# Two rows of each sum on ScalarE, and the first stores behind the last load, in a row-wise dot product with softmax

## The chip, the cores and the metric

The kernel runs on one core of one Trainium2 chip. The metric is the device time of one execution in microseconds (us). A profile gives the span of one profiled execution, which is about 2 us shorter than its device time. Times quoted are medians of runs.

## The reference

```python
B, N, D = 8, 4096, 512                                # x, y: float32
gram = np.matmul(x, y.transpose(0, 2, 1))
diag = np.diagonal(gram, axis1=1, axis2=2)            # only row n of x with row n of y
diag = diag - diag.max(axis=-1, keepdims=True)
exp = np.exp(diag)
return (exp / exp.sum(axis=-1, keepdims=True)).astype(np.float32)
```

Only the diagonal is needed: 8 x 4096 dot products of length 512, then a softmax over 4096 of them, eight times. All of x and y is read once, 134.2 MB; the output has 131 KB.

## The kernel before

The 8 rows of the output are done as two sets of four. Each set is four steps of 32 rows a partition, eight steps in all. x has two buffers, y has one. In the first six steps (`S - 2`) VectorE multiplies all rows with two instructions and sums them with a third. ScalarE's only large work there is a copy of the last six rows of y, so that the y buffer is free as soon as the first product ends. The last two steps use fused multiply-and-sum instructions row by row, with ever smaller loads.

```python
    # R = 32 rows a step, K = 6, C // R = 4 steps a set, G = 32, P = 128
    for t in range(S - 2):
        load_x(t, 0, R)                      # waits for the sum of step t - 2
        load_y(t, 0, R)                      # waits for the first product of step t - 1
        nc.scalar.activation(out=side, in_=ys[:, R - K :, :], func=Act.Copy)
        products(t, 0, R - K, ys[:, : R - K, :])
        if t == C // R:
            store(0, sump, G)                # first set: sum, reciprocal, scale, four stores
        products(t, R - K, K, side)
        sums(t, 0, R)                        # one VectorE reduce of 32 rows
        if t == C // R - 1:
            sump = exps(0, diag[0])
    # ... step 6: y in two halves, fused dots; step 7: loads of 16, 8, 4, 2, 1, 1 rows, fused dots ...
    store(1, exps(1, diag[1][:, C - 2 :]), P)

    def store(i, sump, n):
        # ... total, reciprocal, scaling on VectorE ...
        for p in range(0, P, n):
            nc.scalar.dma_start(out=ov[i, p : p + n, :], in_=res[i][p : p + n, :])
```

All loads are issued by SP, the SyncE engine, in program order. An issue puts a load into SP's queue; the load lands when its last byte is in the buffer.

Of the kernel before, what the change touches and what calls it, by code (L numbers as in the profile page):

```python
# [1 line left out]

# [5 lines left out]


@with_exitstack
def kernel(
    ctx: ExitStack,
    tc: tile.TileContext,
    x: bass.AP,
    y: bass.AP,
    out: bass.AP,
):
    nc = tc.nc
    ctx.enter_context(tc.manual_schedule())  # L20
    f32 = mybir.dt.float32
    Alu = mybir.AluOpType
    Act = mybir.ActivationFunctionType
    X = mybir.AxisListType.X
    B, N, D = x.shape
    P = nc.NUM_PARTITIONS
    G = 32
    Q = P // G
    C = N // G
    R = 32  # L30
    H = R // 2
    K = 6
    S = B // Q * (C // R)


    xv = x.rearrange("(s b) (j c) d -> s (b j) c d", b=Q, j=G)
    yv = y.rearrange("(s b) (j c) d -> s (b j) c d", b=Q, j=G)
    ov = out.rearrange("(s b) (j c) -> s (b j) c", b=Q, j=G)

    big = ctx.enter_context(tc.tile_pool(name="big", bufs=1))  # L40
    small = ctx.enter_context(tc.tile_pool(name="small", bufs=1))


    xs = [big.tile([P, R, D], f32, name=f"xs{i}") for i in range(2)]
    ys = big.tile([P, R, D], f32, name="ys")
    side = big.tile([P, K, D], f32, name="side")

    diag = [small.tile([P, C + 2 * i], f32, name=f"diag{i}") for i in range(B // Q)]
    res = [small.tile([P, C], f32, name=f"res{i}") for i in range(B // Q)]

    def columns(t, r0, n):
        c0 = t % (C // R) * R + r0
        return slice(c0, c0 + n)

    def rows(t, r0, n):
        return xs[t % 2][:, r0 : r0 + n, :]

    def dots_of(t, r0, n):
        return diag[t * R // C][:, columns(t, r0, n)]

    def load_x(t, r0, n):
        nc.sync.dma_start(out=rows(t, r0, n), in_=xv[t * R // C, :, columns(t, r0, n), :])  # L62

    def load_y(t, r0, n):
        nc.sync.dma_start(out=ys[:, r0 : r0 + n, :], in_=yv[t * R // C, :, columns(t, r0, n), :])  # L65

    def products(t, r0, n, yt):
        xt = rows(t, r0, n)
        nc.vector.tensor_tensor(out=xt, in0=xt, in1=yt, op=Alu.mult)  # L69

    def sums(t, r0, n):
        nc.vector.tensor_reduce(out=dots_of(t, r0, n), in_=rows(t, r0, n), axis=X, op=Alu.add)  # L72

    def dots(t, r0, n):
        for r in range(r0, r0 + n):
            xt = xs[t % 2][:, r, :]
            nc.vector.scalar_tensor_tensor(  # L77
                out=xt, in0=xt, scalar=1.0, in1=ys[:, r, :], op0=Alu.mult, op1=Alu.mult,
                accum_out=dots_of(t, r, 1),
            )  # L80

    def over_quadrant(name, column, op, negate=False):

        got = small.tile([P, 1], f32, name=name)
        nc.vector.tensor_reduce(  # L85
            out=got, in_=column.to_broadcast([P, G]), axis=X, op=op, negate=negate, apply_transpose=True
        )
        return got

    def largest(out, d):  # L90
        nc.vector.tensor_reduce(out=out, in_=d, axis=X, op=Alu.max)  # L91

    def exps(i, d):
        mxp = small.tile([P, 1], f32, name=f"mxp{i}")
        largest(mxp, d)
        nmx = over_quadrant(f"nmx{i}", mxp, Alu.max, negate=True)
        sump = small.tile([P, 1], f32, name=f"sump{i}")
        nc.scalar.activation(out=res[i], in_=diag[i][:, :C], func=Act.Exp, bias=nmx, scale=1.0, accum_out=sump)  # L98
        return sump

    def store(i, sump, n):
        total = over_quadrant(f"sum{i}", sump, Alu.add)
        rc = small.tile([P, 1], f32, name=f"rc{i}")
        nc.vector.reciprocal(out=rc, in_=total)  # L104
        nc.vector.tensor_single_scalar(out=res[i], in_=res[i], scalar=rc, op=Alu.mult)  # L105
        for p in range(0, P, n):
            nc.scalar.dma_start(out=ov[i, p : p + n, :], in_=res[i][p : p + n, :])

    for t in range(S - 2):
        load_x(t, 0, R)  # L110
        load_y(t, 0, R)
        nc.scalar.activation(out=side, in_=ys[:, R - K :, :], func=Act.Copy)  # L112
        products(t, 0, R - K, ys[:, : R - K, :])
        if t == C // R:
            store(0, sump, G)
        products(t, R - K, K, side)
        sums(t, 0, R)
        if t == C // R - 1:
            sump = exps(0, diag[0])

    t = S - 2
    load_x(t, 0, R)
    for r0 in (0, H):
        load_y(t, r0, H)
        dots(t, r0, H)

    t += 1
    r0 = 0
    for n in (16, 8, 4, 2, 1, 1):
        load_x(t, r0, n)  # L130
        load_y(t, r0, n)
        if r0 == 0:
            largest(diag[1][:, C : C + 1], diag[1][:, : C - R])
        if r0 == R - 2:
            largest(diag[1][:, C + 1 :], diag[1][:, C - R : C - 2])
        dots(t, r0, n)
        r0 += n
    store(1, exps(1, diag[1][:, C - 2 :]), P)


# [1 line left out]
_INS = ['x', 'y']  # L142
_OUTS = [((8, 4096), 'float32')]


# [23 lines left out]
```

## Time and profile before

| | before |
|---|---|
| three runs | 321.05 to 321.68 us, median 321.35 |
| span of the profiled run | 319.5 us |
| VectorE busy | 249.1 us (78%) |
| ScalarE busy | 18.9 us (6%) |
| load queue's share of the 16 DMA engines | 97.6% |
| one step | 38.7 us, 16.78 MB, 433 GB/s |

### The profile page before, as it was taken

What the parts mean: (1) busy time and instruction counts of PE and PEld (TensorE: products, weight loads), DVE (VectorE), ACT (ScalarE), POOL (GpSimd) and SP (SyncE); (2) the same over time, 40 slices, a digit from 0 to 9 for tenths busy, and PEclk for the clock granted to TensorE, in tenths of its full rate; (3) what the DMA queues carried; (4) which work ended last, traced back from release to release, by engine and by line L of the source; (5) the groups of instructions that cost most, each with busy time, mean ns of one, the idle gap of its engine ahead of it and who ended that gap; (6) DMA issues with size and microseconds to landing.
All of it is one profiled execution on the core that took longest, in us unless ns stands there. A gap on an engine that the chain in (4) does not pass through costs nothing.

```text
span 319.5 us, 284 instructions
## 1 busy us (share of the span) xinstructions
DVE 249.1 (78%) x158; ACT 18.9 (6%) x11; POOL 0.2 (0%) x4
## 2 busy tenths in 40 slices
DVE  0000079996899949999499995999959999994995
ACT  1000030000300003000120003000030000000000
POOL 0000000000000000000000000000000000000000
DMA  9999999999999999999999999999999999999992
GB/s 394 394 394 517 402 394 484 435 394 468 435 410 394 492 427 394 484 435 394 435 476 402 394 509 410 394 492 429 396 414 484 390 419 447 415 431 410 424 411 101
DMA packets 4225, 134.36 MB, mean 421 GB/s; under 512 B 512, under 2 KB 768, under 8 KB 1536
## 3 DMA queue, kind: packets, MB, share of 16 engines
q1 hardware_dynamic: 3888, 134.22, 97.6%
q10 hardware_dynamic: 336, 0.13, 0.1%
q14 instruction: 1, 0.01, 0.0%
HBM read 134.22 MB, written 0.13 MB: 421 GB/s over the span
## 4 chain that ended last, share of the span: by engine, by line
DMA 60%; DVE 36%; issue 2%; SPq 0%; ACT 0%; DVEq 0%
DMA ys<-in_y_dram 60%; DVE xs L69 27%; DVE xs L77 5%; DVE diag L72 4%; SPq L62 0%; DVE res L105 0%; DVE sum L85 0%; DVE nmx L85 0%; ACT res L98 0%; DVE rc L104 0%; DVE mxp L91 0%; SPq L65 0%; DVEq L69 0%; DVEq L77 0%
## 5 line engine op out<-in xcount | busy, mean ns | idle before, releaser
L69 DVE TENSOR_TENSOR xs<-xs,ys 128x13312 f32<-128x13312 f32 x6 | 84.2, 14025 | 62.3 <-DMA ys<-in_y_dram 62.3
L72 DVE TENSOR_REDUCE diag<-xs 128x32 f32<-128x16384 f32 x6 | 103.3, 17220 | 0.2
L77 DVE SCALAR_TENSOR_TENSOR xs<-xs,ys 128x512 f32<-128x512 f32 x64 | 39.6, 685 | 4.6 <-DMA ys<-in_y_dram 4.5
L112 ACT ACTIVATE side<-ys 128x3072 f32<-128x3072 f32 x6 | 16.6, 2765 | 187.5 <-DMA ys<-in_y_dram 151.4
L69 DVE TENSOR_TENSOR xs<-xs,side 128x3072 f32<-128x3072 f32 x6 | 20.1, 3351 | 0.0
L98 ACT ACTIVATE res<-diag,nmx 128x128 f32<-128x128 f32 x2 | 0.8, 402 | 109.2 <-DVE nmx L85 109.2
L77 DVE DVE_READ_ACCUMULATOR xs<-xs,ys 128x1 f32 x64 | 5.2, 81 | 0.0
L112 ACT ACT_TABLE_LOAD x1 | 1.3, 1283 | 0.7 <-PEq L153 0.7
L85 DVE TRANSPOSE_TENSOR_REDUCE sum<-sump 128x1 f32<-128x32 f32 x2 | 0.4, 208 | 0.6 <-ACT res L98 0.6
L105 DVE TENSOR_SCALAR res<-res,rc 128x128 f32<-128x128 f32 x2 | 0.6, 287 | 0.1
L91 DVE TENSOR_REDUCE mxp<-diag 128x1 f32<-128x128 f32 (+1 forms) x2 | 0.4, 222 | 0.1
L91 DVE TENSOR_REDUCE diag<-diag 128x1 f32<-128x96 f32 (+1 forms) x2 | 0.4, 218 | 0.1
L85 DVE TRANSPOSE_TENSOR_REDUCE nmx<-mxp 128x1 f32<-128x32 f32 x2 | 0.4, 212 | 0.1
L104 DVE RECIPROCAL rc<-sum 128x1 f32<-128x1 f32 x2 | 0.3, 164 | 0.1
L98 ACT ACTIVATION_READ_ACCUMULATOR res<-diag,nmx 128x1 f32 x2 | 0.4, 187 | 0.0
L153 POOL MEMSET const-uint8-127<- 128x1 uint8 x1 | 0.1, 103 | 0.0
L153 POOL MEMSET const-bfloat16-1.0<- 128x1 bf16 x1 | 0.1, 102 | 0.0
L153 POOL MEMSET const-float32-0.0<- 128x1 f32 x1 | 0.1, 99 | 0.2 <-issue 0.2
L153 POOL MEMSET const-float32-1.0<- 128x1 f32 x1 | 0.1, 99 | 0.0
## 6 DMA issues: line engine op xcount, KB each, us to landing
ys<-in_y_dram SPq DMA_DIRECT2D x3, 4096.0 KB, 14.9
xs<-in_x_dram SPq DMA_DIRECT2D x1, 4096.0 KB, 14.1
xs<-in_x_dram SPq DMA_DIRECT2D x1, 2048.0 KB, 18.5
ys<-in_y_dram SPq DMA_DIRECT2D x1, 2048.0 KB, 18.9
xs<-in_x_dram SPq DMA_DIRECT2D x1, 1024.0 KB, 21.0
ys<-in_y_dram SPq DMA_DIRECT2D x1, 1024.0 KB, 21.4
xs<-in_x_dram SPq DMA_DIRECT2D x1, 512.0 KB, 22.3
ys<-in_y_dram SPq DMA_DIRECT2D x1, 512.0 KB, 22.8
```

The lines of the kernel that those rows point to most:

```text
L69: nc.vector.tensor_tensor(out=xt, in0=xt, in1=yt, op=Alu.mult)
L72: nc.vector.tensor_reduce(out=dots_of(t, r0, n), in_=rows(t, r0, n), axis=X, op=Alu.add)
L77: nc.vector.scalar_tensor_tensor(out=xt, in0=xt, scalar=1.0, in1=ys[:, r, :], op0=Alu.mult, op1=Alu.mult, accum_out=dots_of(t, r, 1),)
L85: nc.vector.tensor_reduce(out=got, in_=column.to_broadcast([P, G]), axis=X, op=op, negate=negate, apply_transpose=True)
L91: nc.vector.tensor_reduce(out=out, in_=d, axis=X, op=Alu.max)
L98: nc.scalar.activation(out=res[i], in_=diag[i][:, :C], func=Act.Exp, bias=nmx, scale=1.0, accum_out=sump)
L104: nc.vector.reciprocal(out=rc, in_=total)
L105: nc.vector.tensor_single_scalar(out=res[i], in_=res[i], scalar=rc, op=Alu.mult)
L112: nc.scalar.activation(out=side, in_=ys[:, R - K :, :], func=Act.Copy)
L153: nc = _bacc.Bacc("TRN2", target_bir_lowering=False, num_devices=1)
```

## The change

Its intent is to take work off VectorE, so that x buffers come free earlier, and to take the four small stores of the first set out of the stream of loads, to a place behind it.

```diff
+    W = 2
...
+    def sums_act(t, r0, n):
+        for r in range(r0, r0 + n):
+            row = xs[t % 2][:, r, :]
+            nc.scalar.activation(out=row, in_=row, func=Act.Copy, accum_out=dots_of(t, r, 1))
...
-    def store(i, sump, n):
+    def normalize(i, sump):
         # ... total, reciprocal, scaling as before ...
-        for p in range(0, P, n):
-            nc.scalar.dma_start(out=ov[i, p : p + n, :], in_=res[i][p : p + n, :])
...
         if t == C // R:
-            store(0, sump, G)
+            normalize(0, sump)
         products(t, R - K, K, side)
-        sums(t, 0, R)
+        sums(t, 0, R - W)
+        sums_act(t, R - W, W)
...
-    store(1, exps(1, diag[1][:, C - 2 :]), P)
+
+    for p in range(0, P, G):
+        nc.sync.dma_start(out=ov[0, p : p + G, :], in_=res[0][p : p + G, :])
+    normalize(1, exps(1, diag[1][:, C - 2 :]))
+    nc.scalar.dma_start(out=ov[1], in_=res[1])
```

## The prediction

> **What bounds the kernel now.** I read the page first for who is busy, then the windows for the rate of the loads step by step, then the timeline of one step for when loads are issued and land, then the waits of the load queue, then the tail.
>
> The page's parts 2, 3 and 5, of the kernel before. The queue rows give packets, MB and the share of 16 engines' span; the group rows give busy time, mean ns of one, and idle time ahead of it.
> ```profile
> DMA  9999999999999999999999999999999999999992
> ...
> q1 hardware_dynamic: 3888, 134.22, 97.6%
> q10 hardware_dynamic: 336, 0.13, 0.1%
> ...
> L69 DVE TENSOR_TENSOR xs<-xs,ys 128x13312 f32<-128x13312 f32 x6 | 84.2, 14025 | 62.3 <-DMA ys<-in_y_dram 62.3
> L72 DVE TENSOR_REDUCE diag<-xs 128x32 f32<-128x16384 f32 x6 | 103.3, 17220 | 0.2
> L112 ACT ACTIVATE side<-ys 128x3072 f32<-128x3072 f32 x6 | 16.6, 2765 | 187.5 <-DMA ys<-in_y_dram 151.4
> ```
> The load queue q1 occupies the 16 DMA engines for 97.6% of the span, and the DMA row is full until the last slice. VectorE is 78% busy, and the big product waits for a y load in every one of its six steps. Every input byte is read once, 134.22 MB, so traffic cannot shrink.
>
> The windows of the six steps from the first product on (stretch, its us, VectorE busy, ScalarE busy, GpSimd busy, clock, DMA share, GB/s):
> ```profile
> 42.15:80.85 38.70, 34.52 (x3) 2.73 (x1) 0.00 (x0) 1.00 1.01 434
> 80.85:119.86 39.01, 34.51 (x3) 2.77 (x1) 0.00 (x0) 1.00 0.99 430
> 119.86:158.58 38.72, 34.51 (x3) 2.77 (x1) 0.00 (x0) 1.00 1.00 433
> 158.58:197.29 38.71, 35.01 (x5) 3.26 (x3) 0.00 (x0) 1.00 1.00 433
> 197.29:236.16 38.87, 35.08 (x6) 2.76 (x1) 0.00 (x0) 1.00 1.00 433
> 236.16:274.85 38.69, 38.61 (x16) 2.77 (x1) 0.00 (x0) 1.00 0.98 424
> ```
> A step takes 38.7 us whatever VectorE does in it: 34.5 us of work or 38.6. The DMA share is 1.00. A step moves 2 x 128 x 16384 x 4 bytes = 16.78 MB, and 16.78 MB / 38.7 us = 433 GB/s. The loads set the pace.
>
> What could still starve them is a late issue. The timeline of one step (start us, duration us, instruction):
> ```profile
> 56.30 0.33 SPq L65 DMA_DIRECT2D ys<-in_y_dram  x1
> 59.52 17.22 DVE L72 TENSOR_REDUCE diag<-xs 128x32 f32<-128x16384 f32 x1
> 76.77 0.33 SPq L62 DMA_DIRECT2D xs<-in_x_dram  x1
> ...
> 80.90 14.03 DVE L69 TENSOR_TENSOR xs<-xs,ys 128x13312 f32<-128x13312 f32 x1 [4.16 <-DMA ys<-in_y_dram]
> ```
> The next x load is issued at 76.77, when the sum is done; the y load ahead of it in the queue lands just before 80.9. So the queue holds about 4 us of work when the x load joins it. The y load is issued at 56.30 and takes 24.5 us to land, where its own 8.39 MB need 19.4 us at 433 GB/s: it too joined while some 5 us of the earlier x load was left. The chain of waits calls 36% of the span VectorE, but that is the path of issues, which has slack of 4 to 5 us in every step; the share of the DMA engines is the bound. The waits of the load queue name the sum (100.6 us for five x loads), yet those waits are hidden behind transfers.
>
> **What the Trainium skill says.** "DMA: Bandwidth & Descriptors", section Specifications, puts the fabric ceiling of one core's 16 DMA engines at 435 GB/s. The trace agrees: 433 to 434 GB/s in steady steps, so no better arrangement of issues can make these loads faster. The same page, section "Queues, rings and completion order", says that SP and ACT own one row each on the same 16 engines, which serve rows in turn, and that descriptors of one row are consumed in ring order. So stores issued by SP after the last load stand behind it, while the old ones on ScalarE's row were mixed into the stream. The trace shows the mixing: a store took 18.1 us (median) to land in mid-stream and 1.6 us in the idle queue at the end. "ScalarE: Activation LUTs", section "What ACT_TABLE_LOAD costs", gives an activation with immediate scale and bias 186 ns + 0.833 ns per element, so 2745 ns for 3072 elements; this trace has 2765. It gives 613 ns for a row of 512, for which the trace has no record. The section "Table sets" counts copy among the cheap functions that are in every set, so no second table load is due; one is in the trace (1.28 us, hidden under the first load).
>
> **The change part by part.**
>
> *Two rows of each sum go to ScalarE.* VectorE's sum costs 17,220 ns for 32 rows, 538 ns a row; 30 rows should cost 16.14 us, 1.08 us less, and 6.5 us less over six steps. ScalarE gains twelve activations of 128x512 in place, each with an accumulator read (187 ns in the trace). By the skill's formula, an estimate, 0.61 + 0.19 = 0.80 us, 1.6 us a step, 9.6 us in all; ScalarE is idle 36 us ahead of each copy in the steps that were like this. The two start when the small product is done (56.14 + 3.35 = 59.5) and should end by 61.2, some 14 us before VectorE's shorter sum. So the sum on VectorE still releases the next x load, 1.08 us earlier (about 75.7 where it was 76.77). That load then waits 5 us in the queue where it waited 4. Worth on the path: 0. VectorE's idle ahead of each product grows from about 4 to about 5 us.
>
> *The last two steps.* They keep 64 fused rows on VectorE (39.6 us). The sixth sum ends 1.1 us earlier, so the fused rows begin near 269.6 instead of 270.67, and the issues released by them come 1.1 us earlier. VectorE then waits 4.06 us (290.6 to 294.69) for a y load; this wait becomes 5.1 us and takes the gain. Worth: 0.
>
> *The four stores of the first set.* They leave the middle. q10 has 0.1% of 319.5 us, 0.3 us with rounding of half that, for five issues. The step that holds the four stores took 38.87 us, the median of its neighbours 38.71: 0.16 us. The final store alone, with the same 64 KB, shows about 0.23 us of mean engine share. I take 0.2 us out of the stream, so the last load lands 0.2 us earlier.
>
> *Their place in the tail.* Here is the tail before:
> ```profile
> 304.44 0.33 SPq L65 DMA_DIRECT2D ys<-in_y_dram  x1
> ...
> 314.62 0.69 DVE L77 SCALAR_TENSOR_TENSOR xs<-xs,ys 128x512 f32<-128x512 f32 x1 [0.46 <-DMA ys<-in_y_dram]
> ...
> 317.08 0.36 ACTq L107 DMA_DIRECT2D out_dram<-res  x1
> ```
> The last load is issued at 304.44 and lands just before 314.62; the final store goes out at 317.08 and lands 1.6 us later; the span ends at 319.5. Between 313.4 and 317 the engines are idle. SP's last issues each waited for the load eight issues before them to land, as their times 294.66, 299.50 and 304.44 match the landings of the 16-row y and the two 8-row loads. If the four stores follow suit they wait for the 4-row and 2-row loads, which by bytes at 433 GB/s land at 306.9, 309.3, 310.5 and 311.7. They then stand behind the last load and should land 1 to 2 us after it, at 315.5 to 316.5. The last store leaves near 316.9. They fit in the idle stretch with about 1 us in hand, on other work's time. Worth: 0.
>
> Sum: 321.35 - 0.2 = 321.15, which I round to 321.1.
>
> **The rivals.**
> *VectorE is the real bound.* For it: 78% busy, 36% of the chain, and the waits of x loads for the sum. Then 6.5 us come off, about 314.9. Against it: the idle before each product and a DMA share of 1.00. 1%.
> *A hidden bubble in the load queue.* Earlier x loads would fill it, for perhaps 1 us. The rate of 433 against a stated ceiling of 435 leaves 0.5%, 1.5 us, at the very most. 5%, to 320.3.
> *ScalarE takes over the release of the x load.* If a row cost ten times the estimate it would end after VectorE, but 4 us of queue stand behind that. The copies of 3072 elements at 2.77 us speak against it. No effect on time, 2%.
> *The moved stores lengthen the end.* If they delay the last load's landing, or land later than the final store, 0.5 to 2 us are added: 321.7 to 323. For it: a write to memory completes late and four issues wait in turn. Against: the idle stretch above. 10%.
>
> **Range and chances.** The three runs before spread 321.05 to 321.68, so a median moves by some 0.3 us by itself, twice the effect. With the rivals, 8 in 10 lie in 320.4 to 321.9. Two per cent is 6.4 us: only a bound misread by everything above, or an unforeseen wait, gets there. Faster 0.01, same 0.98, slower 0.01.
>
> **What would show it.** VectorE's sum at about 16.1 us x6 and its busy total at 242.6; idle before the big products near 68 us where it was 62.3; x loads issued about 1.1 us earlier but steps still 38.7 us at 433 GB/s; the wait at 290 grown to about 5 us; twelve activations of 0.6 to 0.8 us; the last fused row at 314.4 with the same 5 us behind it; the four stores landed before the final one leaves. It is wrong if steps shorten (VectorE or a bubble mattered), if x loads are released by ScalarE later than y lands, or if the stretch from the last fused row to the end grows.

## The result, and the profile after

The changed kernel took 321.31 us (median of 6 runs, 321.13 to 321.54); the kernel before, in six runs, 321.58 (321.05 to 321.89). The ratio is 0.9994 with a 95% interval of 0.9981 to 1.0007, so: the same.

The page of the changed kernel, its queues (packets, MB, share of 16 engines) and groups (busy, mean ns of one, idle ahead):

```profile
q1 hardware_dynamic: 4080, 134.29, 97.8%
q10 hardware_dynamic: 144, 0.07, 0.1%
...
L70 DVE TENSOR_TENSOR xs<-xs,ys 128x13312 f32<-128x13312 f32 x6 | 84.1, 14025 | 67.1 <-DMA ys<-in_y_dram 67.1
L73 DVE TENSOR_REDUCE diag<-xs 128x30 f32<-128x15360 f32 x6 | 96.9, 16153 | 0.2
...
L78 ACT ACTIVATE xs<-xs 128x512 f32<-128x512 f32 x12 | 7.5, 621 | 88.2 <-DVE xs L70 88.2
...
L78 ACT ACTIVATION_READ_ACCUMULATOR xs<-xs 128x1 f32 x12 | 2.2, 187 | 0.0
```

The four stores moved from q10 to q1, the loads' queue. The sum fell from 17,220 to 16,153 ns, and VectorE's idle time ahead of the big products rose from 62.3 to 67.1 us: most of the 6.4 us saved became waiting. The twelve activations cost 621 ns each.

The timeline of the same step as shown of before (start us, duration us):

```profile
56.36 0.33 SPq L66 DMA_DIRECT2D ys<-in_y_dram  x1
59.58 0.63 ACT L78 ACTIVATE xs<-xs 128x512 f32<-128x512 f32 x1 [14.64 <-DVE xs L70]
59.58 16.15 DVE L73 TENSOR_REDUCE diag<-xs 128x30 f32<-128x15360 f32 x1
...
75.79 0.33 SPq L63 DMA_DIRECT2D xs<-in_x_dram  x1
...
80.94 14.02 DVE L70 TENSOR_TENSOR xs<-xs,ys 128x13312 f32<-128x13312 f32 x1 [5.21 <-DMA ys<-in_y_dram]
```

The x load is issued 0.98 us earlier (75.79 for 76.77), still released by VectorE's sum, and the y load ahead of it lands where it did. The windows by step (us, VectorE, ScalarE and GpSimd busy, clock, DMA share, GB/s):

```profile
80.89:119.59 38.70, 33.45 (x3) 4.10 (x5) 0.00 (x0) 1.00 1.00 434
119.59:158.29 38.70, 33.45 (x3) 4.10 (x5) 0.00 (x0) 1.00 1.00 434
...
197.00:235.70 38.70, 34.01 (x6) 4.07 (x5) 0.00 (x0) 1.00 1.00 434
```

All steps now take 38.70 us. Of before, the second took 39.01 and the fifth 38.87. From the first big product to the sixth, five steps, it is 193.50 us after (42.25 to 235.75) and 194.01 before (42.19 to 236.20). So 0.5 us did go, in this pair of executions. From the sixth product to the end it is 83.4 us after and 83.3 before; the kernel before, profiled again, took 83.6, so no difference is shown there. The spans are 319.2 and 319.5 (319.7 in the second profile of before).

The tail of the changed kernel:

```profile
304.05 0.33 SPq L66 DMA_DIRECT2D ys<-in_y_dram  x1
...
306.48 5.38 SPq L145 DMA_DIRECT2D out_dram<-res  x4
...
314.24 0.69 DVE L83 SCALAR_TENSOR_TENSOR xs<-xs,ys 128x512 f32<-128x512 f32 x1 [0.48 <-DMA ys<-in_y_dram]
...
316.77 0.37 ACTq L147 DMA_DIRECT2D out_dram<-res  x1
```

The four stores are issued between 306.48 and 311.86, behind the last load. Their packets ran from 312.6 to 313.9, so they were done before the final store was issued at 316.77. From the last fused row to the end of the span it is 5.0 us; before it was 4.9.

### The profile page after: what moved, and what is told of

Same layout as the page of the kernel before. It is cut to its first block, busy times and chain, and to the rows that moved or that the text cites. A ratio compares the mean times of both kernels' runs of the same rounds, so it can differ in the third digit from the quotient of the medians.

```text
span 319.2 us, 318 instructions
## 1 busy us (share of the span) xinstructions
DVE 242.8 (76%) x158; ACT 26.9 (8%) x35; POOL 0.2 (0%) x4
## 4 chain that ended last, share of the span: by engine, by line
DMA 61%; DVE 36%; issue 2%; SPq 0%; ACT 0%; DVEq 0%; ACTq 0%
DMA ys<-in_y_dram 61%; DVE xs L70 27%; DVE xs L83 5%; DVE diag L73 4%; SPq L63 0%; DVE res L111 0%; ACT res L104 0%; DVE nmx L91 0%; DVE sum L91 0%; DVE rc L110 0%; DVE mxp L97 0%; SPq L66 0%; DVEq L70 0%; DVEq L83 0%; ACTq L104 0%
## 5 line engine op out<-in xcount | busy, mean ns | idle before, releaser
L70 DVE TENSOR_TENSOR xs<-xs,ys 128x13312 f32<-128x13312 f32 x6 | 84.1, 14025 | 67.1 <-DMA ys<-in_y_dram 67.1
L73 DVE TENSOR_REDUCE diag<-xs 128x30 f32<-128x15360 f32 x6 | 96.9, 16153 | 0.2
L78 ACT ACTIVATE xs<-xs 128x512 f32<-128x512 f32 x12 | 7.5, 621 | 88.2 <-DVE xs L70 88.2
L78 ACT ACTIVATION_READ_ACCUMULATOR xs<-xs 128x1 f32 x12 | 2.2, 187 | 0.0
```

What stands on the lines that cost most here:

```text
L70: nc.vector.tensor_tensor(out=xt, in0=xt, in1=yt, op=Alu.mult)
L73: nc.vector.tensor_reduce(out=dots_of(t, r0, n), in_=rows(t, r0, n), axis=X, op=Alu.add)
L78: nc.scalar.activation(out=row, in_=row, func=Act.Copy, accum_out=dots_of(t, r, 1))
```

## The experiments

The theory on entering: the stream of loads sets the pace, and work taken from VectorE is worth nothing because each x load joins a queue with 4 us of work in it. The rivals: VectorE matters after all; or the two parts cancel, the sums gaining and the stores losing.

**Only the sums moved.**

```diff
-        sums(t, 0, R)
+        sums(t, 0, R - W)
+        sums_act(t, R - W, W)          # stores stay as in the kernel before
```

> The kernel before with two rows of each of the first six sums on ScalarE, the stores left where they were. Theory (the load stream sets the pace and each x load joins a queue with 4 us of work in it): 0.0 us, within 0.3 us of before; idle ahead of the big products near 67 us, x loads issued 1.1 us earlier, steps still 38.7 us. Rival (VectorE bounds the steps): 6.5 us faster. Rival (the two parts cancel: the sums gain, the stores lose): about 0.5 to 1 us faster here.

It took 321.24 us (five runs, 321.22 to 321.43) beside 321.48 for before; ratio 0.9992 (0.998 to 1.0004). VectorE as the bound (6.5 us) is refuted. Its steps are 38.70, 38.71, 38.70, 38.70 and 38.88: the long second step is gone, and the fifth, which holds the four stores, is 0.18 us longer than the others. An issue of this kernel, and the product ahead of it and behind it:

```profile
80.79 14.03 DVE L70 TENSOR_TENSOR xs<-xs,ys 128x13312 f32<-128x13312 f32 x1 [5.22 <-DMA ys<-in_y_dram]
...
114.34 0.33 SPq L63 DMA_DIRECT2D xs<-in_x_dram  x1
...
119.50 14.02 DVE L70 TENSOR_TENSOR xs<-xs,ys 128x13312 f32<-128x13312 f32 x1 [5.22 <-DMA ys<-in_y_dram]
```

The runs do not exclude the lower end of the rival that the parts cancel: 0.5 us faster lies within the interval. The steps put the gain at about 0.3 us, and the tail shows no loss through the stores.

**Only the stores moved.**

```diff
-            store(0, sump, G)
+            normalize(0, sump)
         products(t, R - K, K, side)
         sums(t, 0, R)                  # VectorE sums all rows, as before
+    # four stores of the first set by SP, behind the last load
```

> The kernel before with only the four stores of the first set moved behind the last load; all sums on VectorE. Theory: 0.2 us faster (0.0 to 0.4), the four stores landed before the final store leaves near 316.9. Rival (the moved stores lengthen the end): 0.5 to 2 us slower, with a longer stretch between the last fused row and the end. Rival (parts cancel): slower by what the sums alone gain.

The median was 321.78 us, but the six runs were uneven: 321.28, 322.27, 321.16, 323.47, 322.93 and 320.87. The ratio of 1.0019 has an interval of 0.9994 to 1.0043, so it settles nothing. The profiled run has the tail of the changed kernel, and five steps of 194.18 us with a second step of 39.06. It was run again, last below.

**Sixteen rows on ScalarE.**

```diff
-    W = 2
+    W = 16
```

> The changed kernel with 16 rows instead of two of each sum on ScalarE. By the changed kernel's trace a row takes ScalarE 0.63 us from start to start, so 16 take about 10.2 us against 8.6 us for VectorE's 16 rows: ScalarE now releases the x load, about 6.7 us earlier than before. Theory: time as the changed kernel within 0.3 us, VectorE busy falls by about 45 us, idle ahead of the big products grows by about 6 us a step. Rival (earlier x loads or a freer VectorE are worth something): several us faster, eight times what two rows gave.

321.48 us (321.38 to 321.55), ratio 0.9998. VectorE's busy time fell to 197.5 us, and the first such x load went out at 68.08, against 75.79 with two rows and 76.77 before. It bought nothing more. The guess that ScalarE would release the load was wrong: ScalarE began its rows at 94.90 in the second step, right after the big product and 3.15 us before VectorE's sum, because those in its first part were complete by then.

**No store of the first set at all.**

```diff
-        for p in range(0, P, n):
-            nc.scalar.dma_start(...)   # for the first set, nowhere; its half of the output is not written
```

> The kernel before without any store of the first set (half of the output is left unwritten, so the result is wrong on purpose). It gives the most that moving the stores could ever be worth. Theory: 0.2 us faster than before (0.0 to 0.4), the same as the run with only the stores moved, because behind the last load they cost nothing. Rival (the moved stores lengthen the end): faster than the run with only the stores moved by 0.5 us or more.

321.46 us (321.19 to 321.76), ratio 0.9998 (0.9986 to 1.001). Its output is wrong, which doesn't matter for the time. The whole cost of the four stores is below what runs can resolve. Its fifth step took 38.70 us, but its second 39.11, and five steps 193.90: the long second step has nothing to do with the stores.

**Four rows summed twice on VectorE.** This puts work on the part that was held to have 4 us to spare.

```diff
+        sums(t, 0, 4)
         sums(t, 0, R)
```

> The kernel before with four rows of each of the first six sums computed twice on VectorE, 2.15 us of VectorE work a step at 538 ns a row; the result stays right. Theory (4 us of slack at each x load): no change, within 0.4 us; x loads issued 2.1 us later, idle ahead of the products down to about 2 us a step. Rival (VectorE's time counts in part or whole): up to 13 us slower.

It was 6.8 us slower: 328.19 us (326.08 to 330.79), ratio 1.0237 (1.0178 to 1.0296). The profiled execution is the quickest of the four, 326.08 us; what made the others up to 4.7 us longer was not caught in a profile. The theory of 4 us of slack fell here. The rival that VectorE's time counts as such did not fit either: VectorE was busy for 36.7 us of a step. The windows by step, then one issue and the product after it:

```profile
42.15:80.85 38.70, 36.71 (x4) 2.74 (x1) 0.00 (x0) 1.00 1.00 428
80.85:120.94 40.09, 36.71 (x4) 2.76 (x1) 0.00 (x0) 1.00 0.99 423
120.94:159.66 38.72, 36.71 (x4) 2.76 (x1) 0.00 (x0) 1.00 1.01 430
159.66:199.94 40.28, 37.21 (x6) 3.26 (x3) 0.00 (x0) 1.00 0.97 420
199.94:238.99 39.05, 37.28 (x7) 2.76 (x1) 0.00 (x0) 1.00 1.00 428
```
```profile
78.98 0.33 SPq L62 DMA_DIRECT2D xs<-in_x_dram  x1
80.90 14.03 DVE L69 TENSOR_TENSOR xs<-xs,ys 128x13312 f32<-128x13312 f32 x1 [1.95 <-DMA ys<-in_y_dram]
```

VectorE works the same 36.71 us in the first three, yet the second takes 1.4 us more. The x load was issued at 78.98, 1.9 us before the product that marks the landing of the y load ahead, and the step after it is long. As that step was long, its own x load came 3.3 us ahead of the next landing (issued at 117.67, product at 120.99), and the step after that is 38.72 again. So lateness of the issue costs time well before 4 us of it are used up. The lead alone does not set the length of a step, though: 3.3 us here gave 38.72, while 4.1 us in the kernel before gave 39.01. Where the DMA share stays near 1.00 while GB/s falls from 430 to 423, engines are counted as busy in packets that take longer.

The trace records every DMA packet (the piece of a load that one DMA engine moves at a time) with its duration, so I counted. No view of the profile shows these counts. A packet of 64 KB takes 2.42 us (median). Longer than 2.50 us, after the first 10 us of the span, were:

| kernel | 64 KB packets over 2.50 us | excess over the median, per engine | five steps |
|---|---|---|---|
| before | 25 | 0.32 us | 194.01 us |
| before, profiled again | 15 | 0.17 us | 193.94 us |
| only the stores moved | 21 | 0.33 us | 194.18 us |
| only the stores moved, again | 35 | 0.45 us | 193.94 us |
| no first store | 21 | 0.41 us | 193.90 us |
| four rows summed twice | 67 | 1.90 us | 196.84 us |
| only the sums moved | 0 | 0 | 193.69 us |
| changed kernel | 0 | 0 | 193.50 us |
| changed, stores last of all | 0 | 0 | 193.50 us |
| sixteen rows | 2 | 0.05 us | 193.75 us |

Before, nearly all of the long packets start where an x load takes over from the y load ahead of it (79.7 to 80.5, 118.4, 157.3, 196, 235.5 us). In the kernel with four rows summed twice they take 2.8 to 3.2 us in the worst places, like the very first packets of each kernel, which start from an empty queue. Every kernel that issues x loads 1 us earlier than before has none there. The two of the sixteen-row kernel, at 99.5 and 240.5 us, each follow an 8 KB instruction fetch, at 99.2 and 240.2, on the same 16 engines. The excess is a mean over the engines and does not order the kernels with late issues: 0.17 and 0.45 us both stand beside 193.94.

The table takes 64 KB packets alone, so it says nothing of the last two steps' smaller loads. There the changed kernel has one packet well over its median: 1.88 us where a 32 KB packet takes 1.22, starting 0.3 us after an instruction fetch at 274.52. Every one of the 16 such fetches during the loads of the 14 profiles is followed by a packet lengthened in this way.

The landings tell the same of the 16 engines' parts of one load. Before, they are 0.78 to 0.80 us apart (first to last) in the first two loads of x and of y, 1.07 us in the third x load, and 0.94 to 1.03 in the other loads of the first six steps. After, they stay at 0.76 to 0.80 through the first six steps. Before, some engine had fallen behind by about 0.3 us, and a product waits for the last engine. After the fetch at 274.52 the changed kernel's parts spread too, from 0.75 to 1.09 us.

**Fifteen rows summed twice.**

```diff
+        sums(t, 0, 15)
         sums(t, 0, R)
```

> The kernel before with 15 rows of each of the first six sums computed twice on VectorE, 8.07 us a step. Theory: the slack of about 4 us is used up and VectorE becomes the bound, so steps take 34.5 + 8.1 = 42.6 us, five of them 3.9 us longer each and the last steps about 4 us longer: about 24 us slower, 345 us (338 to 350). Rival (VectorE never matters, the queue holds far more than 4 us): no change. Rival (all VectorE time counts already): 48 us slower.

349.11 us, ratio 1.086 (1.0844 to 1.0877): slower by 27.7 us, inside neither rival and at the upper edge of the range. Steps took 42.5 to 43.1 us, and five of them 19.8 us more than before, as expected. The last two steps took 91.0 us from the sixth product to the end of the span, 7.7 more than before where 4 were expected. So there too nearly all of the 8.07 us counted, and the 4.06 us that VectorE idled before did not absorb them.

**Lighter loads, before and after the change.** Both kernels have the same edit, which makes the result wrong and VectorE the longest part of the first six steps.

```diff
+    for part in (xs[0], xs[1], ys):
+        nc.gpsimd.memset(part[:, 24:R, :], 1.0)
     for t in range(S - 2):
-        load_x(t, 0, R)
-        load_y(t, 0, R)
+        load_x(t, 0, 24)
+        load_y(t, 0, 24)
```

> The kernel before with only 24 of the 32 rows of x and y loaded in each of the first six steps, the other rows set to one once at the start (wrong result on purpose, all arithmetic kept). A step's loads then take 29.0 us at 433 GB/s, less than VectorE's 34.5 us. Theory: VectorE becomes the bound, steps of about 34.6 us, total about 288 us (283 to 295).

> The changed kernel with the same lighter loads. Theory: with VectorE the bound, each of the first six sums is worth its 1.08 us, so steps of about 33.5 us and 6.5 us (5 to 7.5) less than the lighter kernel before. Rival (moving two rows never helps, because ScalarE or the y buffer holds the step): within 1 us of the lighter kernel before.

They took 293.91 (293.81 to 294.03) and 288.99 us (288.84 to 289.18), so the change is worth 4.9 us here, just under the 5 to 7.5 forecast. The same steps of both, before ahead of after:

```profile
66.90:101.40 34.50, 34.47 (x5) 2.76 (x1) 0.00 (x0) 1.00 0.86 365
101.40:135.85 34.45, 34.42 (x4) 2.76 (x1) 0.00 (x0) 1.00 0.86 365
```
```profile
66.00:99.40 33.40, 33.37 (x4) 3.99 (x5) 0.00 (x0) 1.00 0.89 377
99.40:132.80 33.40, 33.37 (x5) 3.99 (x5) 0.00 (x0) 1.00 0.89 377
```

VectorE is busy for all of a step, the DMA share is down to 0.86, and each of these steps is shorter by 1.05 to 1.10 us, about the 1.07 us that the sum lost. So the edit does what it is meant to do where VectorE is the bound. It brings 5.1 us by the sixth product (205.94 and 200.82), not 6.5 in the end, because the last two steps load all rows again: from the issue of the seventh x load (206.09 and 201.05) the stream is the bound, and the sixth sum's 1.07 us vanishes. My 288 for the first was a slip of addition: from 206.09 on, 33.6 MB are left, 77.5 us at 433 GB/s, which alone gives 283.6 for the last byte.

**The moved stores after the final store.**

```diff
-    # four stores by SP, behind the last load
     nc.scalar.dma_start(out=ov[1], in_=res[1])
+    for p in range(0, P, G):
+        nc.scalar.dma_start(out=ov[0, p : p + G, :], in_=res[0][p : p + G, :])
```

> The changed kernel with the four stores of the first set issued by ScalarE after the final store, so that they no longer stand in the idle stretch. Theory (they are free only because they end before the final store leaves): the four issues of 0.43 us each move the last landing, 1.5 to 2.5 us slower than the changed kernel, about 323.2 us. Rival (a few small stores cost nothing anywhere): no change.

322.83 us (322.76 to 322.86), 1.5 us over the changed kernel's median, spans 321.0 and 319.2; ratio to before 1.004 (1.0023 to 1.0057). The final store left at 316.82, as in the changed kernel, and four issues of 1.86 us in all followed at 317.24. The four stores cost nothing behind the last load because they end there in a stretch in which the rest is waited for.

**The kernel before, profiled again.** No edit.

> The kernel before, profiled once more. In the first profile of it two steps took 39.01 and 38.87 us where the others took 38.7, and the second of the two held the stores. If the stores caused the 0.16 us, the fifth step is long again and the second is not; if both were accidents of one execution, other steps or none are long.

The fifth step is long again (38.87 us) and so is the second (38.89). Neither was an accident. The fifth is long in the three profiles with stores inside and plain packets otherwise (38.87, 38.87 and 38.88), and 38.70 in the changed kernel and in four others without stores there. One profile does not fit: the first of only the stores moved has no store in its fifth step and took 38.99 us, with one packet of 3.58 us at 196.0. The second is long in all five profiles of kernels with the original sum (38.89 to 39.11).

**Four rows summed twice, with x loads in halves.** By now a new theory stood: what counts is how long before the end of the load ahead an x load is issued.

```diff
-        load_x(t, 0, R)
+        load_x(t, 0, H)
+        load_x(t, H, H)
...
-        sums(t, 0, R)
+        sums(t, 0, 4)
+        sums(t, 0, H)
+        sums(t, H, H)
```

> The run with four rows summed twice on VectorE was 6.8 us slower, although VectorE still had 2 us of idle time a step. Here VectorE does the same extra work, but the sum is cut into two of 16 rows and each x load of the loop into two halves, so the first half is issued when 16 rows are summed, 8.6 us before the second. New theory (only the time between the issue of an x load and the end of the load ahead of it counts, and 4 us of it is just enough): back to before within 0.4 us, about 321.4 us, with no lengthened packets. Rival (the extra VectorE work itself costs time): 326 to 330 us as in the run without the cut.

322.81 us (322.45 to 324.05) beside 321.8 for before, ratio 1.004 (1.0018 to 1.0062). The windows of the two steps answer to those of the kernel without the halves:

```profile
80.77:119.44 38.67, 36.77 (x5) 2.76 (x1) 0.00 (x0) 1.00 1.01 434
119.44:158.32 38.88, 36.77 (x5) 2.76 (x1) 0.00 (x0) 1.00 1.00 432
```

VectorE does as much in a step, 36.77 us, and the five steps take 194.03 us for 196.84: the loop's whole loss is back. No packet of 64 KB in it took over 2.50 us, as forecast, and after the first 10 us none of the 32 KB packets of the loop took over 1.23 (1.21 is the median). The halves also made the x packets 32 KB instead of 64; this run does not separate that from the earlier issue. Total time is not within the 0.4 us forecast. The rest, 1.5 us between the profiles, is in the last two steps, where the 16-row y load is released by fused rows and so was issued at 282.70 instead of 280.57; the rate from 280 to 290 us was 396 GB/s for 416 before. Between 283.7 and 285.0 us 14 packets of 32 KB took 1.6 to 2.1 us. That fits lateness again, in a load that the halves did not help.

**Only the stores moved, again.**

> The kernel with only the stores moved, once more: its six runs spread from 320.87 to 323.47 us where the changed kernel kept within 0.4 us. If moving the stores alone makes time uneven, several runs lie above 322 us again and the others near 321. If it was an accident of that series, all runs lie within 321.0 to 322.0 us as those of the kernel before. By the new theory x loads issued as late as before are exposed to small losses, so runs above those of the changed kernel are expected, at most a few tenths.

321.3 us (321.03 to 321.82), ratio 0.9989 (0.9972 to 1.0006), so the runs above 322 did not come back, while before reached 322.73 in this series. The rival that the moved stores lengthen the end by 0.5 us or more is refuted: the interval ends 0.2 us above before. What made single runs of the earlier series 1 to 2 us longer was not caught in a profile and stays open. The runs of the changed kernel, of only the sums moved and of sixteen rows, 16 in all, lie between 321.13 and 321.55 us. That fits the lost packets as a source of the spread, but does not show it.

## Why the prediction was right or wrong

**The bound: right.** The stream of loads sets the pace. Sixteen rows off VectorE bought no more than two; the same edit with lighter loads bought 4.9 us.

**The sums' own numbers: right.** 16,153 ns for 16.14 us; 621 ns a row for 613 (with the accumulator read a row took 0.63 us from start to start, not the 0.80 estimated, because the two overlap); one table load again, as forecast; VectorE busy 242.8 us for 242.6; idle ahead of the products 67.1 for 68; the wait near 290 us 5.04 for 5.1.

**The worth of the earlier x load: mis-sized, and for a wrong reason.** The prediction said that the path of issues "has slack of 4 to 5 us in every step", that the load "then waits 5 us in the queue where it waited 4", and "Worth on the path: 0". Measured is about 0.3 us over five steps (194.01 and 193.94 before, 193.69 with only the sums moved). The 4 us were not all slack: 2.15 us of them taken away in each step, 10.75 in five, cost 2.8 us in the five steps. The rival of a hidden bubble, dismissed at 5%, was right in kind and a third of its guess in size.

**The last two steps: right in result, wrong in reason.** From the sixth product to the end it is 83.4 us after, 83.3 and 83.6 before, so the 1.1 us brought nothing that shows. But "this wait becomes 5.1 us and takes the gain" treated the wait as spare time. Delay VectorE by 2.15 us and 1.3 to 1.7 us of it show (84.9 us in both runs that did so); the wait does not absorb it.

**The stores: right.** I took 0.2 us; the fifth step shows 0.17 to 0.18, and the five steps 0.19 with the shorter sum (193.69 to 193.50). With the original sum no gain shows over five steps: 193.90, 193.94 and 194.18 without the stores, 194.01 and 193.94 with them. Their place in the tail was right too, with issues between 306.48 and 311.86 where 306.9 to 311.7 was worked out; they were done by 314.3, earlier than the 315.5 to 316.5 expected. One line was misread: 18.1 us is the median landing of all five stores, the final one among them; for the four in mid-stream it is 20.4. Stores issued later than the final one cost 1.5 us.

**The sum.** 0.2 us for the stores was forecast; about 0.5 left the loop (0.4 by the second profile of before), and the medians fell by 0.27 us, from 321.58 to 321.31. Runs alone cannot tell this from zero; the step times and packets show the gain in the loop. That 0.27 lies so near 0.2 is luck: 0.3 us from the earlier x loads was not forecast, and the spread of the runs is as large.

## What to carry to other kernels

The time between a load's issue and the end of the load ahead of it is not all spare. Delay an issue on purpose and watch the rate before calling such a wait hidden. When the stream is the bound, moving arithmetic to another engine is worth only what it repairs in the stream: here that was 0.3 us of 321, and sixteen rows brought no more than two.

## What the Trainium skill lacked or had wrong

- "DMA: Bandwidth & Descriptors" does not say how early the next load must be issued to keep the rate. Here an issue 4.1 us before the product that marks the landing of the load ahead left packets of up to 3.0 us at the change-over (3.3 in the second profile), where 2.42 us is the median; issues 4.5 to 5.2 us before, in the changed kernel, left none; 1.9 us before cost 1.4 us in the step after. Why packets at a late change-over take longer, no run shows.
- No page gives what an instruction fetch costs a data load on the same engines (it belongs to the same page, or to "Runtime: NRT & Kernel Launch"). In the sixteen-row kernel two fetches of 8 KB were each followed 0.3 us later by one packet of 2.76 or 2.80 us where the median is 2.42, and after the first the parts of the load landed 1.15 us apart instead of 0.77. All 16 fetches during the loads of the 14 profiles have such a packet behind them.
- "ScalarE: Activation LUTs" has no figure for the accumulator read behind an activation: 187 ns here. Rows of 512 followed each other every 0.61 to 0.63 us with it: in the changed kernel the read ran from 60.11 to 60.30, over the start of the next activation at 60.21.
